# GpSimd's work after the first stage on VectorE, and the softmax products on ScalarE, in a hybrid S5 and attention encoder

## The chip, the cores and the metric

The kernel runs on one core of a Trainium2 chip. The core has five engines with a queue each that is worked off in order: TensorE (PE in the profile; PEld are its weight loads), VectorE (DVE), ScalarE (ACT), GpSimd (POOL) and SyncE (SP), which mostly starts DMAs. Engines wait for each other by semaphores. The metric is the device time of one execution in microseconds, the median of the runs. Lower is better.

## The reference

The input x has 256 tokens of 2048 channels in float32. The trunk has two layers. Layer 0 mixes tokens with a bidirectional S5 state-space mixer that ends in a gated linear unit, `(z @ w_glu_a) * sigmoid(z @ w_glu_b)`. Layer 1 mixes them with grouped-query attention in a window of 128 tokens: 32 query heads of 64 channels share 4 key and value heads, queries and keys are RMS-normalised and rotated, and each head has a sink logit in its softmax. After each mixer follows a squared-ReLU MLP of width 8192. Each of the four parts is `h = h + part(rms_norm(h))`. Cut to the attention core, which matters most here:

```python
qkv = h @ w_qkv
q = apply_rotary(head_rms_norm(q, q_gain), positions)
k = apply_rotary(head_rms_norm(k, k_gain), positions)
scores = einsum(q, k) * 64 ** -0.5, masked to |i - j| <= 128
m = max(max(scores), sink)
p = exp(scores - m)
denom = sum(p) + exp(sink - m)
out = einsum(p / denom, v) @ w_o
```

## The kernel before

Tokens lie on the 128 partitions, in two tiles (`tt` 0 and 1). The residual stays in SBUF (`resid`). All four large parts of the network are matmuls whose weights stream in from HBM once, 1 MB at a time.

*Matmuls in three passes.* A float32 product is made of three fast ones: each operand is split into a rounded high part and the rest, and `mm3` (L717 to L719) adds high x high, low x high and high x low. So each weight tile (`wload`, L665) goes through three steps: a DMA on SyncE's queue into one of two raw buffers; a cast to the high part on ScalarE (L679); and a subtraction that gives the low part (L680). There are three buffers each for high and low parts. The table `whow` (L1289), filled from `QH`, `UH` and `OH` (L39 to L41), says for each tile into how many pieces it is cut and which engine subtracts: each letter is a piece, "v" on VectorE and "g" on GpSimd. In the attention's first product (`QH`, 20 tiles) every other tile from the sixth on is one whole piece on GpSimd; one of the first five tiles of the MLP behind the gated unit (`UH`) is four pieces on GpSimd. The tiles of the gated unit that are named by `WP` are on GpSimd too, and the change leaves them there.

*Norms.* The RMS norm is spread out: `norm_pre` (L731) multiplies a 512-wide block of the residual by the gain (L735) while ScalarE squares and sums it (L737); `norm_post` (L739) transposes the block on PE (L744) and splits it into high and low (L747); the factor 1/rms comes later, from `norm_end`. The gain product is on GpSimd, but for four blocks at the end of the first MLP, for which the caller passes VectorE. `glu_post` (L807) does this for the gated unit, after a sum (L816, L817), the gate (L820, L822) and the residual's sum (L823). At the end of the attention, `fin` (L1262) does it after the residual's sum (L1267).

*Attention.* `proj` (L1179) runs the projection of one head group, 8 query heads at a time with 512 columns: 16 steps of six matmuls, four weight tiles. The keys and values come first, then four groups (`mains`, L1241), then the output projection. While the next group is projected, the heads of the one before run in nine stages for each half of the tokens, at steps given by `HS` (L28). The stages of one half in `attn_head` (L1104):

- `rot`: squares (L1095), their sums and the rsqrt (`head_r`), then the rotary products on VectorE (L1086, L1087) and their sum on GpSimd (`rope`, L1088);
- `turn`: four transposes on PE (L1119), copied by ScalarE (L1121);
- two times `scores`: matmuls (L1130); VectorE adds the mask and finds the maxima (L1134);
- `soft`: maxima and sink (L1143 to L1146, VectorE), eight exponentials with their sums (L1149, ScalarE), the sums' reciprocals (L1150, L1151, VectorE), and eight products of the exponentials with them (L1153, VectorE), 128x256 each;
- `flip` and `mix`: per pair of heads, four transposes of the weights on PE (L1159), a copy by ScalarE (L1161), then the products with the values (L1168); after the last pair the result is split by ScalarE and VectorE (L1173, L1174).

Of the copies by L1161, two buffers exist for each half. PE takes its instructions in order, so a `mix` that waits for its copy holds up the projection matmuls behind it.

*What sets the order.* The code gives an order, but a scheduler in the build then sorts the instructions of each engine by a timeline of its own. So an edit in one place can move instructions of other engines. GpSimd and ScalarE also start DMAs: GpSimd four sums into the residual in each MLP half (L951 to L958) and the loads of the attention's small tables (L1059).

Of the kernel before, what the change touches and what calls it, by code (L numbers as in the profile page):

```python
# [35 lines left out]
WP = range(9, 33)  # L36
WD = 20 + 16 + 64 + 64
FAST = (range(2, 27, 3), (0, 4, 7, 10, 13, 16, 20, 23, 26))
QH = ("v", "vv", "vv", "v") + ("vv", "g") * 8  # L39
UH = ("vv", "vv", "gggg", "vv", "vv")  # L40
OH = ("v",) * 16  # L41


# [134 lines left out]
class Kernel:  # L178
# [549 lines left out]
        self.nc.sync.dma_start(gain, self.gain_src[:, cb * 512:(cb + 1) * 512])  # L728
        return gain

    def norm_pre(self, cb, tt, gain, hg, e=None):  # L731

        nc = self.nc
        r = self.resid[:, tt, cb * 512:(cb + 1) * 512]
        (e or nc.gpsimd).tensor_mul(hg, r, gain)  # L735
        sq = self.tmp.tile([P, 512], F32, name="sq")
        nc.scalar.activation(sq, r, AF.Square, accum_out=self.ss[:, tt, cb:cb + 1])  # L737

# [105 lines left out]
    def mlp(self, nxt, fin):  # L844
        nc, ar = self.nc, self.ar
# [53 lines left out]
        v = nc.vector  # L899
# [34 lines left out]
        def fast(a, w, first, end):  # L934
            for bk, j, g, c in LATE if first else FORMS:
                mm(bk, a, j, w[g], c, stop=end and bk[0] != "x")
# [23 lines left out]
        def end(half, t, j):  # L960
            cb = half * 2 + j
            cs = slice(cb * 512, (cb + 1) * 512)
            v.tensor_add(self.resid[:, t, cs], self.resid[:, t, cs], bks["x%d" % (2 * t + j + 1)])
            if last:
                nc.sync.dma_start(self.d["out"][:, t, cs], self.resid[:, t, cs])
            elif half:
                scaled(t, cb, nc.gpsimd)
                if j:
                    self.norm_end(t)

        def scaled(t, cb, e):
            self.norm_pre(cb, t, gains[:, cb * 512:(cb + 1) * 512], hx[:, t, cb], e)

        atail += [ar.get("at#%d" % i, [1024], F32R, at=49664 + 1024 * i) for i in range(2)]
        nx = split(0, False, True)
# [7 lines left out]
        for half in range(2):  # L983
            bks, begun = {}, set()
            pend = []
            for kp in range(NK):
                a = nx
                if half == 0 and kp == 2:
                    ar.free("at")
                    self.wr[0].add(ar.get("wx#49664", [2048], at=49664))  # L990
                if half and kp == NK - 4:
                    for r in self.wr:
                        r.drop()
                    ar.free("wx")
                    atail[:] = [ar.get("at#%d" % i, [1024], F32R, at=49664 + 1024 * i) for i in range(2)]
                if kp + 1 < NK:
                    nx = split(kp + 1, kp + 1 in FAST[half], kp == 0 if not half else kp + 1 >= NK - 2)
                elif not half:
                    nx = split(0, 0 in FAST[1])
                w = self.wnext() if half or kp else w0  # L1000
                if half and kp == 19 and not last:
                    ar.free("hT#0")
                    hx = ar.get("hx", [2, 4, 512], at=31744)
                    gains = ar.get("hg", [D], at=35840)
                    nc.sync.dma_start(gains, self.d["gains"][nxt])
                    self.ss = self.small.tile([P, 2, 4], F32, name="ss")
                    for t in range(2):
                        for cb in range(2):
                            scaled(t, cb, v)
                if kp in FAST[half]:  # L1010
                    fast(a, w, not begun, kp == FAST[half][-1])
                    if kp == FAST[half][-1]:
                        fold()
                elif kp < NK - 1 - half:
                    for b in range(4):
                        plain(a, w, b)
                else:
                    pend.append((a, w))
            if half:
                ar.free("hT", "af")  # L1020
                if not last:
                    self.act = ar.get("act", [KT, 2, L], F32R, at=23552)
            n = half and not last
            for t in range(2):
                for p in pend[:n]:
                    for j in range(2):
                        plain(*p, 2 * t + j)
                for j in range(2):
                    for p in pend[n:]:
                        plain(*p, 2 * t + j, stop=p is pend[-1])  # L1030
                    end(half, t, j)
# [46 lines left out]
    def rope(self, pool, src, n, x, tt):  # L1078

        v = self.nc.vector  # L1080
        t1 = pool.tile([P, n, 2, 32], F32, name="rp_a") if n == 8 else self.tmp.tile([P, n, 2, 32], F32, name="gain")
        t2 = pool.tile([P, n, 2, 32], F32, name="rp_b", bufs=1) if n == 8 else self.tmp.tile([P, n, 2, 32], F32, name="sq")
        sv = src.rearrange("p (n s c) -> p n s c", n=n, s=2)
        A = self.ropeA[:, x, tt].rearrange("p (o s c) -> p o s c", o=1, s=2).broadcast_to([P, n, 2, 32])
        B = self.ropeB[:, x, tt].rearrange("p (o s c) -> p o s c", o=1, s=2).broadcast_to([P, n, 2, 32])
        v.tensor_mul(t1, sv, A)  # L1086
        v.tensor_mul(t2, sv[:, :, ::-1], B)  # L1087
        self.nc.gpsimd.tensor_add(t1, t1, t2)  # L1088
        return t1.rearrange("p n s c -> p (n s c)")

    def head_r(self, pool, src, n, tt, scale, name):
# [12 lines left out]
    def attn_head(self, pool, g, banks):  # L1104

        nc, v, a, pe = self.nc, self.nc.vector, self.nc.scalar, self.nc.tensor
        kT, vt = self.kT, self.vt

        def stages(tt):
# [27 lines left out]
            def soft():  # L1137
                mx, sm = s["mx"], s["sm"]
                snk = self.sink[:, g * 8:(g + 1) * 8]
                nm = self.small.tile([P, 8], F32, name="nm")  # L1140
                es = self.small.tile([P, 8], F32, name="es")
                den = self.small.tile([P, 8], F32, name="den")
                v.tensor_mul(mx, mx, s["r"])  # L1143
                v.tensor_max(mx, mx, snk)
                v.tensor_scalar_mul(nm, mx, -1.0)
                v.tensor_add(es, snk, nm)  # L1146
                a.activation(es, es, AF.Exp)
                for h in range(8):
                    a.activation(sm[:, h], sm[:, h], AF.Exp, scale=s["r"][:, h:h + 1], bias=nm[:, h:h + 1], accum_out=den[:, h:h + 1])  # L1149
                v.tensor_add(den, den, es)  # L1150
                v.reciprocal(den, den)  # L1151
                for h in range(8):
                    v.tensor_scalar_mul(sm[:, h], sm[:, h], den[:, h:h + 1])  # L1153

            def flip(hp):
                bk = self.bank()
# [129 lines left out]
    def run(self):  # L1286
        nc, d, ar = self.nc, self.d, self.ar
        self.wq = []
        self.whow = {**{163 - j: h for j, h in enumerate(QH)}, **{143 - j: h for j, h in enumerate(OH)}, **{291 - j: h for j, h in enumerate(UH)}}  # L1289
        self.wsrc = ([d["wge"][c, k] for c in (1, 2, 3, 0) for k in range(KT // 2)] + [None] + [d["wgl"][c, k] for c in range(4) for k in range(KT // 4)]  # L1290
# [219 lines left out]
```

## Time and profile before

| what | value |
|---|---|
| median of three runs | 2092.61 us (2088.96 to 2093.38) |
| profiled execution | 2089.93 us, its span 2088.1 us |
| PE busy | 2013.2 us (96%) |
| VectorE busy | 1476.5 us (71%) |
| ScalarE busy | 1091.0 us (52%) |
| GpSimd busy | 338.5 us (16%) |
| HBM read | 360.05 MB, 173 GB/s over the span |

The stages in the timeline: the S5 mixer to about 200 us, the gated unit to about 390, the first MLP to about 1095, the attention to about 1390, the second MLP to the end.

In the rows of the profile, "L680 DVE TENSOR_TENSOR slot<-slot,slot" is the work of line 680 on VectorE, output before the arrow. In the timeline the first number is the start in us from the span's start, the second the time until the last of the row's instructions ended; a bracket at the end tells how long the engine stood idle before and what ended that. Successive instructions of one engine overlap a little, so that the distance of two starts is often shorter than a duration. Matmuls of 512 columns last 0.39 us in the rows while starting 0.227 us apart. In a table of waits a row gives the waiting line, what it waited for, the total in us, the number of times and the longest.

### The profile page before, as it was taken

To read this page: it belongs to the slowest core of one execution; us is meant where nothing else is said; L and a number is where in the kernel's file an instruction comes from. 1 tells how busy PE (TensorE), PEld (TensorE's weight loads), DVE (VectorE), ACT (ScalarE), POOL (GpSimd) and SP (SyncE) were. 2 spreads that over 40 slices of the span, in tenths; PEclk is the share of its full clock that TensorE was granted. 3 is DMA by queue.
4 is the path that set the end of the run, shared out by engine and by line. 5 is a ranking of instruction groups with operands and counts; after the bars stand their busy time and mean duration, and the time that the engine had idled before them with its cause. 6 is when DMAs were issued, how large, how long until landed. Compare 5 with 4: busy or idle time off the path is not lost.

```text
span 2088.1 us, 33141 instructions
## 1 busy us (share of the span) xinstructions
PE 2013.2 (96%) x13736; PEld 1693.2 (81%) x13736; DVE 1476.5 (71%) x2096; ACT 1091.0 (52%) x1314; POOL 338.5 (16%) x260
## 2 busy tenths in 40 slices
PE   5989999899999999999999889999999999999999
PEld 4877778788888888878787667888888888787887
DVE  8899636755555578988886877465555557898886
ACT  5553645444444455655554556454444445565553
POOL 6988721200000000000022430100000000000000
PEclk9999999999999999999999999999999999999999
DMA  3224455455555555465564332455555555547554
GB/s 120 71 98 145 153 194 200 166 197 187 196 182 193 191 196 207 181 222 207 198 206 172 121 121 81 149 186 200 193 190 184 197 185 198 204 182 241 182 205 158
DMA packets 61990, 368.47 MB, mean 176 GB/s; under 512 B 7072, under 2 KB 9408, under 8 KB 21904
## 3 DMA queue, kind: packets, MB, share of 16 engines
q1 hardware_dynamic: 54144, 342.32, 46.0%
q10 hardware_dynamic: 5184, 19.49, 2.7%
q0 software_dynamic: 2512, 4.56, 1.2%
q8 instruction: 107, 1.75, 0.3%
q14 instruction: 43, 0.35, 0.0%
HBM read 360.05 MB, written 2.10 MB: 173 GB/s over the span
## 4 chain that ended last, share of the span: by engine, by line
PE 62%; DVE 9%; DMA 7%; ACT 3%; issue 2%; POOL 0%; SPq 0%; ACTq 0%; DVEq 0%
PE bank L858 22%; PE bank L924 22%; PE bank L860 12%; DMA slot<-in_wdn 4%; DVE slot L680 4%; PE bank L717 2%; PE bank L718 1%; PE bank L719 1%; ACT slot L679 1%; DVE slot L694 1%; ACT slot L693 1%; DMA slot<-in_wup 1%; DMA slot<-in_wo 1%; ACT slot L1149 1%; PE bank L1168 1%
## 5 line engine op out<-in xcount | busy, mean ns | idle before, releaser
L680 DVE TENSOR_TENSOR slot<-slot,slot 128x2048 fp32r<-128x2048 f32 (+1 forms) x285 | 628.8, 2209 | 417.2 <-ACT slot L679 414.6
L679 ACT CAST slot<-slot 128x2048 fp32r<-128x2048 f32 (+2 forms) x321 | 554.6, 1733 | 466.5 <-PE bank L858 195.1
L924 PE MATMUL bank<-slot,slot 128*128 128x512 f32 x2124 | 493.4, 390 | 2.5 <-DVE slot L918 1.8
L858 PE MATMUL bank<-slot,slot 128*128 128x512 f32 x2048 | 492.4, 392 | 2.8 <-DVE slot L747 1.6
L924 PEld LDWEIGHTS bank<-slot,slot 128*128 128x128 f32 x2124 | 397.7, 188 | 88.4 <-DVE slot L918 4.2
L858 PEld LDWEIGHTS bank<-slot,slot 128*128 128x128 f32 x2048 | 377.0, 189 | 76.5 <-DVE slot L747 2.2
L860 PEld LDWEIGHTS bank<-slot,slot 128*128 128x128 f32 x2048 | 263.1, 191 | 10.3
L860 PE MATMUL bank<-slot,slot 128*128 128x256 f32 x2048 | 266.3, 283 | 0.0
L717 PE MATMUL bank<-slot,slot 128*128 128x512 f32 x544 | 219.2, 404 | 5.2 <-ACT slot L679 4.9
L719 PE MATMUL bank<-slot,slot 128*128 128x512 f32 x544 | 209.5, 398 | 7.3 <-POOL slot L680 7.1
L718 PE MATMUL bank<-slot,slot 128*128 128x512 f32 x544 | 215.5, 396 | 0.0
L924 PE MATMUL bank<-slot 128*128 128x512 f32 x840 | 201.1, 391 | 4.1 <-DVE slot L918 3.4
L951 POOL DMA_DIRECT2D slot<-slot x4 | 3.7, 921 | 1159.0 <-ACT slot L950 1149.3
L924 PEld LDWEIGHTS bank<-slot 128*128 128x128 f32 x840 | 157.0, 188 | 40.2 <-DVE slot L918 6.5
L694 DVE TENSOR_TENSOR slot<-slot,slot 128x1536 fp32r<-128x1536 f32 x72 | 145.5, 2021 | 39.5 <-ACT slot L693 36.4
L693 ACT CAST slot<-slot 128x1536 fp32r<-128x1536 f32 x72 | 122.3, 1698 | 93.3 <-DMA slot<-in_wdn 46.5
L869 ACT ACTIVATE slot<-slot 128x256 f32<-128x256 f32 x128 | 52.8, 414 | 159.0 <-DVE slot L867 159.0
L717 PEld LDWEIGHTS bank<-slot,slot 128*128 128x128 f32 x544 | 104.0, 191 | 30.0 <-ACT slot L679 6.1
L719 PEld LDWEIGHTS bank<-slot,slot 128*128 128x128 f32 x544 | 102.8, 191 | 31.4 <-POOL slot L680 9.1
L718 PEld LDWEIGHTS bank<-slot,slot 128*128 128x128 f32 x544 | 103.9, 191 | 20.8 <-issue 0.7
L917 ACT CAST slot<-slot 128x512 fp32r<-128x512 f32 (+1 forms) x128 | 90.5, 709 | 53.5 <-PE bank L924 52.9
L680 POOL TENSOR_TENSOR slot<-slot,slot 128x1024 fp32r<-128x1024 f32 (+2 forms) x36 | 100.6, 2808 | 104.6 <-ACT slot L679 98.9
(238 smaller groups left out, 1800.0 us busy)
## 6 DMA issues: line engine op xcount, KB each, us to landing
slot<-in_wup SPq DMA_DIRECT2D x128, 1024.0 KB, 4.9
slot<-in_wdn SPq DMA_DIRECT2D x128, 1024.0 KB, 4.9
slot<-in_wqkv SPq DMA_DIRECT2D x20, 1024.0 KB, 5.0
slot<-in_wge ACTq DMA_DIRECT2D x32, 512.0 KB, 3.8
slot<-in_wgl SPq DMA_DIRECT2D x16, 1024.0 KB, 5.3
slot<-in_wo SPq DMA_DIRECT2D x16, 1024.0 KB, 4.9
slot<-in_bz SPq DMA_DIRECT2D x16, 336.0 KB, 3.3
slot<-in_cp SPq DMA_DIRECT2D x16, 256.0 KB, 2.7
```

The lines of the kernel that those rows point to most:

```text
L679: self.nc.scalar.copy(hi[:, c], raw[:, c])
L680: (self.nc.gpsimd if e == "g" else self.nc.vector).tensor_sub(lo[:, c], raw[:, c], hi[:, c].bitcast(F32))
L693: self.nc.scalar.copy(hi, x)
L694: v.tensor_sub(lo, x, hi.bitcast(F32))
L717: pe.matmul(out, lhsT=xh, rhs=wh, start=first, stop=False)
L718: pe.matmul(out, lhsT=xl, rhs=wh, start=False, stop=False)
L719: pe.matmul(out, lhsT=xh, rhs=wl, start=False, stop=last)
L858: pe.matmul(bk, lhsT=wh[:, kt], rhs=act[:, kt].rearrange("p x c -> p (x c)"), start=(kt == 0), stop=False)
L860: pe.matmul(bk[:, :L], lhsT=wl[:, kt], rhs=act[:, kt, 0], start=False, stop=(kt == KT - 1))
L869: nc.scalar.activation(o if fb % 2 else o[:, ::-1], s.rearrange("p (x c) -> p x c", x=2), AF.Square)
L917: nc.scalar.copy(a[:, :c], h)
L924: pe.matmul(bank(bk), lhsT=a[x][:, j], rhs=w[y][:, c], start=bk not in begun, stop=stop and y == 1)
```

## The change

Three things, all after the first stage (the S5 mixer):

- the subtractions that the tables `QH` and `UH` gave to GpSimd go to VectorE: eight whole tiles of 128x2048 in the attention, and one tile in the gated unit's end that is now cut into two pieces instead of four;
- the gain products (L735, 128x512: eight in the gated unit, four at the first MLP's end, eight at the attention's end) and the rotary sums (L1088: eight of 128x512 and two of 128x256) go from GpSimd to VectorE;
- the 64 products of the exponentials with the reciprocal sums (L1153, 128x256) go from VectorE to ScalarE.

GpSimd keeps in these stages four copies of keys (L1230) and its DMAs.

```diff
-QH = ("v", "vv", "vv", "v") + ("vv", "g") * 8
-UH = ("vv", "vv", "gggg", "vv", "vv")
+QH = ("v", "vv", "vv", "v") + ("vv", "v") * 8
+UH = ("vv", "vv", "vv", "vv", "vv")
...
-    def norm_pre(self, cb, tt, gain, hg, e=None):
+    def norm_pre(self, cb, tt, gain, hg):
...
-        (e or nc.gpsimd).tensor_mul(hg, r, gain)
+        nc.vector.tensor_mul(hg, r, gain)
...
-                scaled(t, cb, nc.gpsimd)
+                scaled(t, cb)
...
-        self.nc.gpsimd.tensor_add(t1, t1, t2)
+        v.tensor_add(t1, t1, t2)
...
-                    v.tensor_scalar_mul(sm[:, h], sm[:, h], den[:, h:h + 1])
+                    a.mul(sm[:, h], sm[:, h], den[:, h:h + 1])
```

More of the change, by code (lines that the diff above doesn't have):

```diff
@@ L966, in end, with scaled @@
             elif half:
-                scaled(t, cb, nc.gpsimd)
+                scaled(t, cb)
                 if j:
                     self.norm_end(t)
-        def scaled(t, cb, e):
-            self.norm_pre(cb, t, gains[:, cb * 512:(cb + 1) * 512], hx[:, t, cb], e)
+        def scaled(t, cb):
+            self.norm_pre(cb, t, gains[:, cb * 512:(cb + 1) * 512], hx[:, t, cb])
         atail += [ar.get("at#%d" % i, [1024], F32R, at=49664 + 1024 * i) for i in range(2)]
@@ L1008, in mlp @@
                         for cb in range(2):
-                            scaled(t, cb, v)
+                            scaled(t, cb)
                 if kp in FAST[half]:
```

## The prediction

> **What bounds the kernel now.** I read the page's busy line first, then the table of waits by engine, then the stage where PE waits most, row by row. One fence after another comes from: the page; a table of stretches (length, then busy time of each engine, granted clock, DMA); PE's waits in four stretches; and the timeline.
>
> ```profile
> PE 2013.2 (96%) x13736; PEld 1693.2 (81%) x13736; DVE 1476.5 (71%) x2096; ACT 1091.0 (52%) x1314; POOL 338.5 (16%) x260
> ```
> ```profile
> 1130.00:1310.00 180.00, 162.75 (x909) 125.15 (x908) 136.11 (x397) 102.90 (x214) 52.12 (x20) 0.94 0.30 109
> ```
> ```profile
> PE bank L717 <- ACT slot L679: 3.5, 1, 3.5
> PE bank L719 <- POOL slot L680: 3.0, 2, 2.0
> PE bank L1119 <- POOL slot L1088: 0.3, 1, 0.3
> ```
> ```profile
> PE bank L1168 <- DVE mx L1134: 4.7, 1, 4.7
> PE bank L1159 <- DVE slot L1153: 4.0, 2, 2.5
> PE bank L719 <- POOL slot L680: 1.0, 1, 1.0
> PE bank L1168 <- ACT slot L1161: 0.4, 1, 0.4
> ```
>
> PE works 96% of the span, so the change can only move the waits of PE. Among the stages it touches, attention holds nearly all: 6.8 us in the first list (1080 to 1180 us) and 10.1 us in the second (1180 to 1320), 16.9 us together. A second loss lies in the granted clock, 0.94 over 180 us: 180 x 0.06 = 10.8 us. It follows waits, as these PE rows show (start, duration): behind the wait of 2.0 us before 1138, projection matmuls start 0.43 us apart; undisturbed, 0.227 us.
>
> ```profile
> 1139.41 0.63 PE L719 MATMUL bank<-slot,slot 128*128 128x512 f32 x1
> 1139.84 0.63 PE L717 MATMUL bank<-slot,slot 128*128 128x512 f32 x1
> ...
> 1260.55 0.39 PE L718 MATMUL bank<-slot,slot 128*128 128x512 f32 x1
> 1260.77 0.39 PE L719 MATMUL bank<-slot,slot 128*128 128x512 f32 x1
> ```
>
> Four waits are 2 us or longer (3.5, 2.0, 4.7, 2.5), so I charge 10.8 / 4 = 2.7 us of slow clock to each, and none to shorter ones. The Trainium skill (TensorE: Matmul & The Clock Gate, What's actually happening) has the clock fall only after an idle window of about 3.4 us; the 2.0 us wait contradicts that here. By its rule only two of the old waits and three of the new ones below would be charged, and the sum at the end would be +3.4 us, not -2.0 us.
>
> Why PE waits is seen on VectorE: the same eight multiplications by reciprocal sums (L1153) take three times as long while GpSimd subtracts.
>
> ```profile
> 1217.53 6.47 DVE L1153 TENSOR_SCALAR slot<-slot,den 128x256 f32<-128x256 f32 x8
> ...
> 1265.22 2.19 DVE L1153 TENSOR_SCALAR slot<-slot,den 128x256 f32<-128x256 f32 x8
> ```
> ```profile
> 1218.98 4.60 POOL L680 TENSOR_TENSOR slot<-slot,slot 128x2048 fp32r<-128x2048 f32 x1 [11.76 <-ACT slot L679]
> ```
>
> The excess, 4.3 us, is about GpSimd's 4.60 us: VectorE stands still meanwhile. Of the 16.9 us only the 2.5 us wait at 1265 (no GpSimd work near it) and the 0.4 us one are free of this; 14.0 us could go.
>
> **The change part by part.** *Subtractions, rotary sums, norm products to VectorE.* Prices (a group of GpSimd rows, then one VectorE row of each size):
>
> ```profile
> L680 POOL TENSOR_TENSOR slot<-slot,slot 128x2048 fp32r<-128x2048 f32 x8 | 38.5, 4811 | 66.2 <-ACT slot L679 66.2
> L735 DVE TENSOR_TENSOR slot<-slot,slot 128x512 f32<-128x512 f32 x4 | 2.5, 684 | 0.0
> ```
> ```profile
> 1226.67 1.22 DVE L680 TENSOR_TENSOR slot<-slot,slot 128x1024 fp32r<-128x1024 f32 x1
> ```
>
> Eight whole-tile subtractions cost VectorE 8 x 2 x 1.22 = 19.5 us at most, eight rotary sums 8 x 0.68 = 5.5 us; they replace GpSimd's 38.5 us for the former alone, during which VectorE was held. Between 1130 and 1310 VectorE was busy 136 us of 180; it loses most of the 52 us that GpSimd held it and the multiplications. So VectorE has room, and in attention I cost this part at nothing; without the cover its 25 us would be the price. The norm products of the layer ends (20 x 0.68 us) fall where PE has other matmuls, but for one place, the end of the gated unit. On VectorE (names: output<-inputs, slot_73 the small ring) before:
>
> ```order
> L816 TENSOR_TENSOR slot_313<-slot_313,bank 128x512
> L822 TENSOR_TENSOR slot_73<-slot_313,slot_73 128x512
> L823 TENSOR_TENSOR slot_73<-slot_73 128x512
> L822 TENSOR_TENSOR slot_73<-slot_313,slot_73 128x512
> L680 TENSOR_TENSOR slot_2734<-slot_82,slot_4069 128x1024
> ```
> and now:
> ```order
> L816 TENSOR_TENSOR slot_313<-slot_313,bank 128x512
> L680 TENSOR_TENSOR slot_2733<-slot_82,slot_4069 128x1024
> L822 TENSOR_TENSOR slot_73<-slot_313,slot_73 128x512
> L680 TENSOR_TENSOR slot_2734<-slot_82,slot_4069 128x1024
> L823 TENSOR_TENSOR slot_73<-slot_73 128x512
> L822 TENSOR_TENSOR slot_73<-slot_313,slot_73 128x512
> L735 TENSOR_TENSOR slot_73<-slot_73 128x512
> ```
>
> Two half subtractions and one more L822 now stand ahead of the first norm product, for which PE's transposes wait (3.94 us below).
>
> ```profile
> 387.48 0.68 DVE L817 TENSOR_TENSOR slot<-slot,bank 128x512 f32<-128x512 f32 x1
> 388.07 0.68 DVE L816 TENSOR_TENSOR slot<-slot,bank 128x512 f32<-128x512 f32 x1
> ```
> ```profile
> 394.18 0.66 PE L744 MATMUL bank<-ident,slot 128*128 128x128 f32 x4 [3.94 <-POOL slot L735]
> ```
>
> From the first L817 to PE: 6.70 us now. After: five short operations at 0.60 apart, a half subtraction 1.2, L822 0.6, another half 1.2, L823 and L822 1.2, L735 0.68 = 7.9 us. **+1.2 us.**
>
> *Multiplications to ScalarE.* ScalarE has such products only 512 wide (L347, the eighth starts 4.3 us after the first, so 0.61 apart); two other ScalarE operations, 512 and 256 wide, differ by 0.21 us.
>
> ```profile
> L347 ACT ACTIVATE slot<-slot,rstd x8: 705/708/722, 65.3 to 69.6; 128x512 f32<-128x512 f32 x8
> ```
> ```profile
> 409.40 0.62 ACT L917 CAST slot<-slot 128x512 fp32r<-128x512 f32 x1
> ...
> 417.33 0.41 ACT L869 ACTIVATE slot<-slot 128x256 f32<-128x256 f32 x1
> ```
>
> So 0.61 - 0.21 = 0.40 us each, 3.2 us for eight (0.50 each if they don't overlap), against 2.19 us on VectorE. What counts is who is behind them. ScalarE in the third head group, first half, before (L1149 exponentials, L679 weight cast, L1095 squares, L1161 copies of transposed weights):
>
> ```order
> L1149 ACTIVATE slot_4602,den<-slot_4602,nm,slot_4603 128x256 x5
> L1095 ACTIVATE slot_73<-bank,rstd 128x512
> L679 CAST slot_4069<-slot_82 128x2048
> L1095 ACTIVATE slot_73<-bank,rstd 128x512
> L1161 COPY slot_4603<-bank 128x512
> ```
> and now:
> ```order
> L1149 ACTIVATE slot_4602,den<-slot_4602,nm,slot_4603 128x256 x5
> L679 CAST slot_4069<-slot_82 128x2048
> L1153 ACTIVATE slot_4602<-slot_4602,den 128x256 x8
> L1095 ACTIVATE slot_73<-bank,rstd 128x512
> L679 CAST slot_4069<-slot_82 128x2048
> L1095 ACTIVATE slot_73<-bank,rstd 128x512
> L1161 COPY slot_4603<-bank 128x512
> ```
>
> The first copy (L1161), which releases the product with the values (L1168) on PE, now stands behind eight products and a second cast. The reciprocals come from VectorE while the first cast runs, so they add no wait. Durations:
>
> ```profile
> 1259.34 0.60 ACT L1149 ACTIVATE slot<-slot,nm,slot 128x256 f32<-128x256 f32 x1 [2.36 <-DVE nm L1145]
> ...
> 1264.12 0.67 ACT L1095 ACTIVATE slot<-bank,rstd 128x512 f32<-128x512 f32 x1
> 1264.69 1.89 ACT L679 CAST slot<-slot 128x2048 fp32r<-128x2048 f32 x1
> 1266.48 0.68 ACT L1095 ACTIVATE slot<-bank,rstd 128x512 f32<-128x512 f32 x1
> 1267.06 1.20 ACT L1161 COPY slot<-bank 128x512 f32<-128x512 f32 x2
> ```
>
> From starts: exponentials 4.78, cast 1.79, products 3.2, square 0.57, cast 1.79, square 0.58, copy 0.58: 13.3 us from the first exponential. On PE, before:
>
> ```order
> L1130 MATMUL bank<-slot_4603,slot_9706 128x256 x8
> L1159 MATMUL bank<-ident,slot_4602 128x128 x8
> L1168 MATMUL bank<-slot_4603 64x128 x4
> L1159 MATMUL bank<-ident,slot_4602 128x128 x8
> L717 MATMUL bank<-slot_4069,slot_9432 128x512
> ```
> and now:
> ```order
> L719 MATMUL bank<-slot_2733,slot_4067 128x512
> L717 MATMUL bank<-slot_4069,slot_4067 128x512
> L718 MATMUL bank<-slot_4069,slot_4067 128x512
> L719 MATMUL bank<-slot_2733,slot_4067 128x512
> L1159 MATMUL bank<-ident,slot_4602 128x128 x8
> L1168 MATMUL bank<-slot_4603 64x128 x4
> L1159 MATMUL bank<-ident,slot_4602 128x128 x8
> ```
>
> Nine projection matmuls now stand between the scores (L1130) and the transposes (L1159), where there were none. PE's durations, from start to start, and when VectorE starts on scores (the trace records each L1130 and L1168 twice, so x16 and x8 there are x8 and x4 in the order):
>
> ```profile
> 1218.03 1.15 PE L1159 MATMUL bank<-ident,slot 128*128 128x128 f32 x8 [1.49 <-DVE slot L1153]
> 1218.94 0.47 PE L719 MATMUL bank<-slot,slot 128*128 128x512 f32 x1
> ...
> 1255.10 0.66 PE L1168 MATMUL bank<-slot,slot 128*64 128x128 f32 x8
> 1255.70 0.66 PE L1119 MATMUL bank<-ident,slot 128*128 128x128 f32 x4
> 1256.11 0.47 PE L717 MATMUL bank<-slot,slot 128*128 128x512 f32 x1
> ...
> 1261.09 2.00 PE L1130 MATMUL bank<-slot,slot 64*128 64x256 f32 x16
> ```
> ```profile
> 1255.38 0.42 DVE L1134 CUSTOM_DVE_ANT_0 slot<-bank,slot 128x256 f32<-128x256 f32 x1
> ...
> 1262.26 0.42 DVE L1134 CUSTOM_DVE_ANT_0 slot<-bank,slot 128x256 f32<-128x256 f32 x1 [2.75 <-PE bank L1130]
> ```
>
> The first exponential came 4.2 us after the end of the scores (1255.10 to 1259.34) with VectorE late; unhindered, VectorE starts 0.8 us before that end (1262.26 against 1263.09) and needs 3.4 (1255.38 to 1259.34, less 0.6 for one operation between), so 2.5 us. I take 3.2, between. The copy is then done 3.2 + 13.3 = 16.5 us after the scores. PE's own work until it wants the copy, with the projection matmuls (0.227 us each) counted in the new order:
> - third group: four L1168 0.60, transposes 0.41, 22 projections 5.0, scores 2.0, nine projections 2.0, transposes 0.91 = 11.0. Wait **5.5**.
> - first: no L1168, 14 projections instead of nine: 11.5. Wait **5.0**.
> - second: one projection more than the first, and L1168: 12.3. Wait **4.2**.
> - fourth: both score sets at once, 41 and 22 projections between: 18.4; ScalarE has 16 exponentials (9.6), products, two casts (3.6), copy: 20.1. Wait **1.7**.
>
> In the first and second the second cast is two halves; I price them as one. New waits 16.4, slow clock 3 x 2.7 = 8.1: 24.5 us, against 16.9 + 10.8 = 27.7. Attention: **-3.2 us**. With the gated unit: **-2.0 us**.
>
> The Trainium skill (ScalarE: Activation LUTs, Rules for kernel authors) would leave products on VectorE. Here 2.19 us against 3.2 us bears it out once GpSimd is out of the way. It speaks against this half of the change: without these products in ScalarE's queue each of the four waits would be up to 3.2 us shorter.
>
> **The rivals.** *The relief carries* (0.28). VectorE's early finish makes the first exponential come sooner and the new waits vanish in PE's slack, all 14.0 us and three slow clocks (8.1) go: -22.1 + 1.2, 2071.7 us. For it: ScalarE was busy only 103 us of 180. Against it: the copy's place in the queue is fixed. *ScalarE becomes the bound* (0.22), the other side. Per group it has 9.6 exponentials, 6.4 products, four casts 7.2, eight copies of about 0.58 and eight more short operations, some 32 us; PE has 96 x 0.227 = 21.8 and twice about 6.5 of attention, some 35. If ScalarE idles for more than those 3 us in a group, the second half's transposes wait too: 3.2 + 2.7 in three groups, +17.7, 2108.3 us. That the change doesn't take GpSimd out cannot be: its rows there are gone but for key copies and DMAs.
>
> **How the numbers follow.** The profiled execution took 2089.93 us (span 2088.1), 2.7 below the median of the runs, 2092.61; I carry the difference of -2.0 over to the median: 2090.6 us. Chance of this case 0.50. Its ends: exponentials at 4.2 instead of 3.2 (+4.0, and a slow clock in the fourth group, +2.7), products at 0.50 (+3.2): 2100.5; exponentials at 2.5 (-2.8), slow clock of 1.8 instead of 2.7, three times: 2085.1. A measurement of this kernel tells no change from about 0.2%, 4.2 us. Case one gives faster 0.09, same 0.36, slower 0.05; the relief 0.26 and 0.02 same; the bound 0.03 same and 0.19. Sum: faster 0.35, same 0.41, slower 0.24. The range takes in case one and reaches into both rivals, 2079 to 2104.
>
> **What would show it.** Right: no GpSimd row in attention but copies and DMAs; VectorE's halves at 1.2 us throughout; PE waiting for L1161 at L1168 three times for 4 to 6 us, and for L735 at the gated unit's end for 5 us. Wrong: these waits missing (relief), or as many again at the second half's L1159 (bound). A clock at 0.97 or more over attention would also say that my charge of 2.7 us was too high.

## The result, and the profile after

The changed kernel takes 2079.09 us, median of 5 runs (2075.13 to 2082.94), against 2092.82 us (2088.96 to 2095.3, 5 runs) for the kernel before: ratio 0.9935, 95% interval 0.9915 to 0.9956. It is 13.7 us faster; 2.0 were forecast, 2090.6 us. The profiled execution of the changed kernel has a span of 2074.6 us, 13.5 less than before, so the two traces show all of the difference. The busy line of its page:

```profile
PE 2004.5 (97%) x13736; PEld 1688.0 (81%) x13736; DVE 1455.1 (70%) x2072; ACT 1116.2 (54%) x1376; POOL 246.1 (12%) x218
```

PE has the same 13736 matmuls as before and is busy 8.7 us less with them; the other 4.8 us are idle time. To find where, I cut both traces at matmuls that occur in both, and took the distances:

| stretch (from, to) | before | after | difference |
|---|---|---|---|
| span's start to first L858 of the first MLP | 385.45 | 384.11 | -1.3 |
| first L858 to first L924 (end of the gated unit in it) | 365.52 | 360.53 | **-5.0** |
| first L924 to the L744 ahead of the attention | 346.44 | 346.75 | +0.3 |
| that L744 to the next one (attention) | 244.70 | 238.39 | **-6.3** |
| that L744 to the last L765 (start of the second MLP) | 54.42 | 53.23 | **-1.2** |
| from there to the end | 691.57 | 691.59 | 0.0 |

The first row is scatter: the fourteen profiles of this study have its end anywhere between 384.1 and 390.3 us. The second repeats better: five of the seven kernels that share the changed kernel's code there have 360.5 us, and the other two (e4 and e8 below) take 1.6 and 1.3 us more, behind a slow clock of which the last section tells. So the stretches in bold can be trusted more than whole times.

*Attention.* Its stretch as a row of the stretches' view, in the kernel before and in the changed one (length, then PE, PEld, DVE, ACT, POOL, the granted clock, DMA share and GB/s):

```profile
1097.41:1342.11 244.70, 227.44 (x1253) 177.48 (x1252) 171.46 (x453) 131.66 (x248) 60.05 (x24) 0.96 0.34 123
```
```profile
1091.39:1329.78 238.39, 223.75 (x1254) 176.38 (x1253) 142.05 (x410) 156.67 (x312) 2.53 (x4) 0.96 0.36 127
```

Read them as length less PE's busy time: PE was idle 17.3 us before and 14.6 after (-2.6), and busy 227.4 and 223.8 with the same matmuls (-3.7). The second part is the slow clock: the same instructions take less time. The clock column, with two digits, is too coarse to show it. By the stretches in which the granted clock is 0.50, PE was busy 19.2 us at half clock before and 12.5 us after; half of the difference is 3.4 us. What PE waits for after the change, from its timeline:

```profile
1167.18 1.13 PE L1168 MATMUL bank<-slot 128*64 128x128 f32 x8 [4.25 <-ACT slot L1161]
...
1209.77 1.13 PE L1168 MATMUL bank<-slot 128*64 128x128 f32 x8 [3.31 <-ACT slot L1161]
...
1252.72 1.13 PE L1168 MATMUL bank<-slot 128*64 128x128 f32 x8 [4.57 <-ACT slot L1161]
...
1298.61 0.66 PE L1168 MATMUL bank<-slot 128*64 128x128 f32 x8 [0.88 <-ACT slot L1161]
...
1309.45 0.66 PE L1168 MATMUL bank<-slot 128*64 128x128 f32 x8 [1.44 <-ACT slot L1161]
```

Every wait behind GpSimd, VectorE's products and the masked scores is gone. In their place stands the one wait that was forecast, the products with the values (L1168) behind the copy (L1161), once in each head group.

*End of the gated unit.* Two rows of PE before, beside the wait of 3.94 us that the prediction shows, and three after:

```profile
394.59 4.58 PE L858 MATMUL bank<-slot,slot 128*128 128x512 f32 x12
...
402.43 1.21 PE L858 MATMUL bank<-slot,slot 128*128 128x512 f32 x4 [1.40 <-DVE slot L747]
```
```profile
384.11 2.88 PE L858 MATMUL bank<-slot,slot 128*128 128x512 f32 x12
...
391.12 0.66 PE L744 MATMUL bank<-ident,slot 128*128 128x128 f32 x4 [2.70 <-DVE slot L735]
391.53 3.00 PE L858 MATMUL bank<-slot,slot 128*128 128x512 f32 x12
```

The wait at L744 fell to 2.70 us, the wait of 1.40 us behind it is gone, and the twelve matmuls after it take 3.00 us, near the 2.88 of undisturbed ones, where they took 4.58 at the slow clock. At the start of the second MLP a wait of 1.21 us, before, has gone as well:

```profile
1388.91 1.20 PE L858 MATMUL bank<-slot,slot 128*128 128x512 f32 x4 [1.21 <-DVE ms L755]
```
```profile
1375.39 1.20 PE L858 MATMUL bank<-slot,slot 128*128 128x512 f32 x4
```

### The profile page after: what moved, and what is told of

It is laid out like the page before. It is cut to its first block, busy times and chain, and to the rows that moved or that the text cites. A ratio compares the mean times of both kernels' runs of the same rounds, so it can differ in the third digit from the quotient of the medians.

```text
span 2074.6 us, 33114 instructions
## 1 busy us (share of the span) xinstructions
PE 2004.5 (97%) x13736; PEld 1688.0 (81%) x13736; DVE 1455.1 (70%) x2072; ACT 1116.2 (54%) x1376; POOL 246.1 (12%) x218
## 4 chain that ended last, share of the span: by engine, by line
PE 69%; DVE 6%; DMA 4%; ACT 4%; issue 2%; DVEq 0%; ACTq 0%
PE bank L858 22%; PE bank L924 21%; PE bank L860 12%; DMA slot<-in_wdn 4%; PE bank L719 4%; PE bank L717 4%; PE bank L718 4%; DVE slot L680 2%; DVE slot L694 1%; ACT slot L1149 1%; ACT slot L693 1%; PE bank L1168 1%; ACT slot L679 1%; PE bank L1159 1%; DVE slot L918 1%
## 5 line engine op out<-in xcount | busy, mean ns | idle before, releaser
L680 DVE TENSOR_TENSOR slot<-slot,slot 128x2048 fp32r<-128x2048 f32 (+1 forms) x295 | 639.4, 2169 | 425.4 <-ACT slot L679 413.2
L679 ACT CAST slot<-slot 128x2048 fp32r<-128x2048 f32 (+1 forms) x319 | 554.5, 1743 | 460.6 <-PE bank L858 190.1
L924 PE MATMUL bank<-slot,slot 128*128 128x512 f32 x2124 | 493.3, 390 | 3.7 <-DVE slot L918 1.9
L858 PE MATMUL bank<-slot,slot 128*128 128x512 f32 x2048 | 490.2, 391 | 0.1
L924 PEld LDWEIGHTS bank<-slot,slot 128*128 128x128 f32 x2124 | 397.8, 188 | 89.6 <-DVE slot L918 4.1
L858 PEld LDWEIGHTS bank<-slot,slot 128*128 128x128 f32 x2048 | 376.0, 188 | 72.8 <-DVE ms L755 0.3
L924 PE MATMUL bank<-slot 128*128 128x512 f32 x840 | 201.1, 391 | 3.1 <-DVE slot L918 2.2
L924 PEld LDWEIGHTS bank<-slot 128*128 128x128 f32 x840 | 156.8, 188 | 39.4 <-DVE slot L918 5.8
L918 DVE TENSOR_TENSOR slot<-slot,slot 128x512 fp32r<-128x512 f32 (+1 forms) x128 | 101.7, 797 | 1.4 <-ACT slot L917 0.7
```

The costliest lines, as they stand in the source:

```text
L679: self.nc.scalar.copy(hi[:, c], raw[:, c])
L680: (self.nc.gpsimd if e == "g" else self.nc.vector).tensor_sub(lo[:, c], raw[:, c], hi[:, c].bitcast(F32))
L858: pe.matmul(bk, lhsT=wh[:, kt], rhs=act[:, kt].rearrange("p x c -> p (x c)"), start=(kt == 0), stop=False)
L918: v.tensor_sub(a[:, n:n + c], h, a[:, :c].bitcast(F32))
L924: pe.matmul(bank(bk), lhsT=a[x][:, j], rhs=w[y][:, c], start=bk not in begun, stop=stop and y == 1)
```

## The experiments

In all of them one place of the code differs from the kernel before or from the changed one. *Queue theory* is the prediction's: in attention, the waits are set by what stands in ScalarE's queue ahead of the first copy L1161, and GpSimd's work held VectorE. Each ratio is to the kernel before on the same chip, with its 95% interval. Stretches are those of the table above.

**e1: GpSimd's work moved, the products left on VectorE** (from the changed kernel).

```diff
-                    a.mul(sm[:, h], sm[:, h], den[:, h:h + 1])
+                    v.tensor_scalar_mul(sm[:, h], sm[:, h], den[:, h:h + 1])
```

> The changed kernel with the eight products (L1153) back on VectorE; all of GpSimd's work stays moved. Queue theory (ScalarE's queue, with 3.2 us of products in front of the first L1161 copy, makes the waits of 14.4 us at L1168): those waits fall to under 6 us in sum, and the kernel takes 2066 to 2073 us, ratio to before 0.988 to 0.9905, against 0.9935 for the change. Rival (the order that the scheduler chooses decides, not who multiplies; VectorE then owes 2.2 us of products ahead of the transposes, L1159): the waits move from L1161 to L1153 with about the same sum of 12 to 16 us, and the ratio stays at 0.9925 to 0.9955.

Measured: 0.9940 (0.9926 to 0.9954), attention 236.8 us: no different from the changed kernel. PE's waits:

```profile
1168.43 0.66 PE L1168 MATMUL bank<-slot 128*64 128x128 f32 x8 [1.22 <-ACT slot L1161]
...
1212.10 1.94 PE L1159 MATMUL bank<-ident,slot 128*128 128x128 f32 x8 [7.47 <-DVE slot L1153]
...
1216.93 1.12 PE L1168 MATMUL bank<-slot 128*64 128x128 f32 x8 [2.90 <-ACT slot L1161]
...
1258.26 0.66 PE L1168 MATMUL bank<-slot 128*64 128x128 f32 x8 [2.06 <-ACT slot L1161]
```

Both theories are half right. In the first and third group PE has as many projection matmuls between scores and transposes as in the changed kernel (14 and 9), and there the wait falls from 4.25 to 1.22 and from 4.57 to 2.06: 3.0 and 2.5 us, a little less than the 3.3 us of the products on ScalarE. In the second group the scheduler now puts none there, where the changed kernel has 14, and PE waits 7.47 + 2.90 us instead of 3.31. The sum of waits, 14.2 us, is near the changed kernel's 14.5.

**e2: only the products moved to ScalarE** (from the kernel before, the reverse of the edit above).

> The kernel before with only the products (L1153) moved to ScalarE; GpSimd keeps its subtractions, rotary sums and norm products. Queue theory: the waits behind GpSimd stay (3.5, 2.0, 1.0, 4.7 us at L679, L680 and L1134), the 4.0 us behind L1153 go, and 8 to 14 us behind L1161 come; ratio 1.000 to 1.006. Rival (freeing VectorE of the products is a gain of its own): fewer waits in sum than the 16.9 us before, ratio 0.994 to 0.998.

Measured: 1.0049 (1.0034 to 1.0064), attention 254.1 us, 9.4 longer. The ratio is the queue theory's, its waits are so in part (a table of PE's waits over attention):

```profile
PE bank L1168 <- ACT slot L1161: 15.0, 5, 9.3
PE bank L1159 <- ACT slot L1153: 3.8, 2, 3.2
PE bank L717 <- ACT slot L679: 3.5, 1, 3.5
PE bank L1119 <- POOL slot L1088: 3.1, 1, 3.1
PE bank L719 <- POOL slot L680: 2.1, 2, 1.1
```

The waits behind L1161 are a little above the 8 to 14 us expected. The 4.7 us behind the masked scores, expected to stay, are gone, and 3.8 us behind the products came. As the prediction had it, this half of the change is a loss by itself, of 9.4 us in attention.

**e3: only attention's GpSimd work moved to VectorE** (from the kernel before).

```diff
-QH = ("v", "vv", "vv", "v") + ("vv", "g") * 8
+QH = ("v", "vv", "vv", "v") + ("vv", "v") * 8
...
-        self.nc.gpsimd.tensor_add(t1, t1, t2)
+        v.tensor_add(t1, t1, t2)
```

> The kernel before with only attention's GpSimd work moved to VectorE (half of the weight subtractions L680 and the rotary sums L1088); products stay on VectorE, the gated unit's end and the norm products stay on GpSimd. Queue theory with VectorE held by GpSimd: 14.0 of the 16.9 us of waits in attention go and most of 10 us of slow clock with them, so attention is 10 to 18 us shorter, ratio 0.991 to 0.995. Rival (VectorE's own 25 us of new work comes out uncovered, or the scheduler's new order makes other waits): attention within 4 us of before, ratio 0.998 to 1.002.

Measured: 0.9972 (0.9961 to 0.9983); attention 238.4 us, 6.3 less than before, between the two expectations. The stretch's row:

```profile
1099.02:1337.41 238.39, 223.22 (x1253) 175.12 (x1252) 158.75 (x471) 132.11 (x248) 5.12 (x6) 0.96 0.36 126
```

Its length is that of the changed kernel: GpSimd's absence alone gives attention's whole gain, and the products on ScalarE add nothing to it. That the two agree to the hundredth is chance, since their waits are others. The relief did not come to 10 us or more since other waits took the place of the old ones: 7.5 us behind the products in the second group, as in e1, and 7.3 us in sum behind L1161.

**e4: only the end of the gated unit and the norm products moved** (from the kernel before). It makes both edits below; **e5** makes the first alone, **e6** the second.

```diff
-UH = ("vv", "vv", "gggg", "vv", "vv")
+UH = ("vv", "vv", "vv", "vv", "vv")
...
-        (e or nc.gpsimd).tensor_mul(hg, r, gain)
+        nc.vector.tensor_mul(hg, r, gain)
```

> The kernel before with only the end of the gated unit (L680 of its last tile) and the norm products (L735) moved to VectorE; attention as before. By the forecast's own step for this place (+1.2 us): ratio 0.9995 to 1.0015. Rival, as the two traces differ outside attention (7.7 us shorter between the first L858 of each MLP and its full speed: 1.2 + 1.6 us of waits and about 1.6 us of slow clock at the first, 1.2 us at the second and what follows from it): ratio 0.995 to 0.9975, attention's waits as before.

> The kernel before with only the four quarter subtractions at the end of the gated unit (third entry of UH) moved from GpSimd to VectorE; norm products stay on GpSimd. Theory A (VectorE stood still while GpSimd subtracted, from 386 to 391 us, and that delayed the gated unit's last operations): most of what e4 showed at that place comes with this edit alone, PE's wait at L744 falls from 3.9 to under 3 us, the stretch from the first L858 to the first L924 from 365.5 to 361 to 363 us, ratio 0.997 to 0.9985. Theory B (the forecast's step: the two half subtractions go ahead of the norm product in VectorE's queue and cost 1.2 us): the wait grows to about 5 us, ratio 1.000 to 1.0015.

> The kernel before with only the norm products (L735) moved from GpSimd to VectorE; the subtractions of UH and attention stay. Theory A: the wait at L744 falls by about the difference of one product, 1.8 against 0.7 us, to 2.5 to 3 us; the second wait there (1.4 us at L858) and the one of 1.2 us at the second layer's start go too; ratio 0.998 to 0.9995. Theory B (it is this half that made e4's gain, since a norm product on GpSimd holds VectorE between the rstd operations): ratio 0.9965 to 0.998, as e4.

Measured: e4 0.9974 (0.9962 to 0.9985), e5 1.0006 (0.9995 to 1.0016), e6 0.9976 (0.9967 to 0.9986). The stretch of the gated unit's end, 365.5 us before, is 362.1 in e4, 366.0 in e5 and 359.7 in e6; attention keeps 244.5 to 245.8. PE at that place in e4, e5 and e6:

```profile
391.11 0.66 PE L744 MATMUL bank<-ident,slot 128*128 128x128 f32 x4 [2.71 <-DVE slot L735]
391.52 4.59 PE L858 MATMUL bank<-slot,slot 128*128 128x512 f32 x12
```
```profile
397.89 1.12 PE L744 MATMUL bank<-ident,slot 128*128 128x128 f32 x4 [4.37 <-POOL slot L735]
398.66 5.34 PE L858 MATMUL bank<-slot,slot 128*128 128x512 f32 x12
```
```profile
392.33 0.66 PE L744 MATMUL bank<-ident,slot 128*128 128x128 f32 x4
392.74 3.01 PE L858 MATMUL bank<-slot,slot 128*128 128x512 f32 x12
...
399.16 1.19 PE L858 MATMUL bank<-slot,slot 128*128 128x512 f32 x4 [1.54 <-DVE slot L747]
```

So at this place the forecast's step falls (e4), and theory B holds in e5 (a wait of 4.37 us, where about 5 were expected) and e6: the norm products alone make the gain. Moving the subtractions alone (e5) gains nothing and costs 0.5 us here; with the norm products on VectorE they bring the wait at L744 back (from none to 2.7) and take the later one of 1.54 away, 0.8 us by the stretch of the changed kernel (360.53 against 359.73).

**e7: each product made twice on ScalarE** (from the changed kernel; the weights are scaled twice).

```diff
-                for h in range(8):
+                for h in [*range(8)] * 2:
                     a.mul(sm[:, h], sm[:, h], den[:, h:h + 1])
```

> The changed kernel with each product (L1153) made twice on ScalarE, so the weights are scaled twice: 3.2 us more in ScalarE's queue for each half of a group. On PE the first half of the first group keeps its order (scores, 14 projection matmuls, transposes, L1168). Queue theory: the wait of 4.25 us there grows by 3.2 us to 7 to 8 us, and the waits for L1161 in sum by 8 to 13 us; ratio to before 0.998 to 1.005. Rival (ScalarE has slack ahead of the copies, what sets the wait is VectorE's softmax operations): that wait stays at 4 to 5 us, ratio 0.993 to 0.996.

Measured: 1.0034 (1.0020 to 1.0047), attention 255.6 us. PE in the first group:

```profile
1167.75 1.97 PE L1159 MATMUL bank<-ident,slot 128*128 128x128 f32 x8 [2.96 <-ACT slot L1153]
...
1177.88 1.13 PE L1168 MATMUL bank<-slot 128*64 128x128 f32 x8 [8.16 <-ACT slot L1161]
```

The 4.25 us have become 2.96 + 8.16, 6.9 more, where 3.2 were expected. ScalarE's queue tells the rest: between the products and the first copy the scheduler has now put the other half's eight exponentials too. Over all of attention the waits behind L1161 grew by only 1 us, to 15.5, where 8 to 13 were expected; 10.0 us behind the products (L1153) and 2.7 us behind a cast came beside them. The rival, slack on ScalarE, falls; but the price of one operation in the queue is not its duration alone.

**e8: casts of every other weight tile on VectorE** (from the changed kernel).

```diff
-QH = ("v", "vv", "vv", "v") + ("vv", "v") * 8
+QH = ("v", "vv", "vv", "v") + ("vv", "w") * 8
...
-                self.nc.scalar.copy(hi[:, c], raw[:, c])
+                (self.nc.vector.tensor_copy if e == "w" else self.nc.scalar.copy)(hi[:, c], raw[:, c])
```

> The changed kernel with the casts (L679) of every other weight tile from the queries on made by VectorE as well, with their subtraction behind. It takes 1.8 us per such tile off ScalarE's queue, where one of them stood in front of the first L1161 copy. Queue theory: the waits for L1161 of 14.4 us in sum fall by about 1.8 us in three groups, to 7 to 11 us, ratio 0.989 to 0.993. Rival (VectorE, with 71 of 130 us busy, becomes late in its turn, or the scheduler puts other ScalarE work into the room): waits of 13 us or more in sum, ratio 0.993 to 0.998.

Measured: 0.9975 (0.9965 to 0.9986), attention 241.2 us. The rival holds: with a cast gone from ScalarE's queue, the scheduler put the other half's eight exponentials (4.8 us) ahead of the first copy in the first two groups, and the waits there grew; in the third, where it did not, the wait fell from 4.57 to 2.96 us. The waits behind L1161 are 17.1 us in sum. The first two groups:

```profile
1175.59 1.13 PE L1168 MATMUL bank<-slot 128*64 128x128 f32 x8 [6.33 <-ACT slot L1161]
...
1219.40 1.13 PE L1168 MATMUL bank<-slot 128*64 128x128 f32 x8 [5.10 <-ACT slot L1161]
```

**e9: the changed kernel with the gated unit's subtractions back on GpSimd** (`UH` as before).

> The changed kernel with the four quarter subtractions at the end of the gated unit (third entry of UH) given back to GpSimd; all else as in the changed kernel. What e5 and e6 show together (norm products on VectorE gain about 5 us there, the subtractions on VectorE then cost some of it): the wait of 2.7 us at L744 goes, the stretch from the first L858 to the first L924 is 1 to 3 us shorter than the 360.5 us of the changed kernel. The scheduler's order in the second group changes too (one projection matmul between scores and transposes, not 14), for which 3 us more of waits are expected there, so the whole comes out near the changed kernel, ratio to before 0.992 to 0.996. Rival (the stretch varies by that much from run to run, and the two edits don't interact): stretch within 0.5 us of 360.5.

Measured: 0.9960 (0.9945 to 0.9975). That stretch is 359.8 us, as in e6, 0.7 less than in the changed kernel: less than expected, nearer the rival. Attention became 4.1 us longer (242.5), by an edit that lies 700 us ahead of it: the scheduler moved 13 projection matmuls away from between scores and transposes in the second group, as the expectation says.

**e10: products of the second half of the tokens back on VectorE** (from the changed kernel).

```diff
-                    a.mul(sm[:, h], sm[:, h], den[:, h:h + 1])
+                    if tt == 0:
+                        a.mul(sm[:, h], sm[:, h], den[:, h:h + 1])
+                    else:
+                        v.tensor_scalar_mul(sm[:, h], sm[:, h], den[:, h:h + 1])
```

> The changed kernel with the products (L1153) of the second half of the tokens back on VectorE, and those of the first half left on ScalarE. PE keeps about the order of the changed kernel in the first halves (14, 12, 8 and 41 projection matmuls between scores and transposes, there 14, 14, 9 and 41). If the order that the scheduler makes decides: the four waits behind L1161 stay at 3 to 5 us each in the first three groups and no wait of 7.5 us behind L1153 comes, ratio to before 0.992 to 0.995. If ScalarE's load as such decides: attention 3 us shorter or more than the changed kernel's, ratio under 0.992.

Measured: 0.9976 (0.9967 to 0.9986), attention 244.7 us. Neither: the first two groups wait 4.25 and 3.72 us as expected, but in the third the scheduler again put the other half's exponentials ahead of the copy:

```profile
1266.41 1.13 PE L1171 MATMUL bank<-slot 128*64 128x128 f32 x8 [9.35 <-ACT slot L1164]
```

**e11: softmax in two parts of four heads, products on VectorE** (from the changed kernel, `UH` as before). **e12: the same two parts, products on ScalarE in the first two groups only** (`UH` as in the changed kernel). The diff is e12's; e11 has its last line for all groups.

```diff
-                for h in range(8):
-                    a.activation(sm[:, h], sm[:, h], AF.Exp, scale=s["r"][:, h:h + 1], bias=nm[:, h:h + 1], accum_out=den[:, h:h + 1])
-                v.tensor_add(den, den, es)
-                v.reciprocal(den, den)
-                for h in range(8):
-                    a.mul(sm[:, h], sm[:, h], den[:, h:h + 1])
+                for q in range(0, 8, 4):
+                    for h in range(q, q + 4):
+                        a.activation(sm[:, h], sm[:, h], AF.Exp, scale=s["r"][:, h:h + 1], bias=nm[:, h:h + 1], accum_out=den[:, h:h + 1])
+                    hs = slice(q, q + 4)
+                    v.tensor_add(den[:, hs], den[:, hs], es[:, hs])
+                    v.reciprocal(den[:, hs], den[:, hs])
+                    for h in range(q, q + 4):
+                        if g < 2:
+                            a.mul(sm[:, h], sm[:, h], den[:, h:h + 1])
+                        else:
+                            v.tensor_scalar_mul(sm[:, h], sm[:, h], den[:, h:h + 1])
```

> The changed kernel with each half's softmax made in two parts of four heads (exponentials, reciprocal sums and products of heads 0 to 3, then of 4 to 7), products on VectorE, and the gated unit's quarter subtractions on GpSimd. The first copy L1161 then stands ahead of one square and one cast more than before in the first group, with no products in ScalarE's queue; in the second group the scheduler has no projection matmul between scores and transposes. Queue theory: first and third group's waits for L1161 under 1.5 us each, the second group's wait behind the softmax 5 to 8 us; attention 233 to 237 us, gated unit's stretch 358 to 360 us, ratio to before 0.989 to 0.992: the best of all. Rival (the sum of waits stays where it is, since the scheduler only moves them): attention 238 us or more, ratio 0.992 to 0.996.

> The changed kernel with each half's softmax made in two parts of four heads, and the products (L1153) on ScalarE in the first two head groups only, on VectorE in the last two. For the first two groups PE keeps the changed kernel's order, with 14 projection matmuls between scores and transposes each; for the last two it has that of e11. If the order of PE and ScalarE's queue together set the waits: about 4.2 and 3.3 us behind L1161 in the first two groups, under 1 us in the third and fourth (there 4.6 and 2.3 us in the changed kernel); attention 229 to 233 us, ratio to before 0.988 to 0.991, the fastest of all. If the scheduler only moves the waits about: attention 236 us or more, ratio 0.992 to 0.996.

Measured: e11 0.9920 (0.9906 to 0.9934), attention 236.1 us; e12 0.9895 (0.9878 to 0.9911), 2070.11 us, attention 228.3 us. PE's waits over attention in e11, as a table, and in e12, with the row of its stretch (line numbers are shifted by the edit: L1161 and L1155 in e11 are transposes and products, L1163 and L1166 the copy, L1170 and L1173 the products with the values):

```profile
PE bank L1161 <- DVE slot L1155: 9.6, 2, 9.3
PE bank L1170 <- ACT slot L1163: 4.8, 1, 4.8
PE bank L1130 <- ACT slot L1121: 0.7, 1, 0.7
```
```profile
PE bank L1173 <- ACT slot L1166: 7.9, 3, 4.3
```
```profile
1095.99:1324.27 228.28, 220.19 (x1254) 174.41 (x1253) 151.94 (x458) 144.77 (x280) 3.14 (x4) 0.99 0.38 133
```

In e11 the first, third and fourth group wait for no copy, as expected; nearly all that is left is the second group, where PE has no projection matmul between scores and transposes: 9.28 + 4.80 us, where 5 to 8 were expected. Its attention is in the range of the queue theory, its ratio at the edge between that and the rival's. e12 gives that group the changed kernel's order and keeps e11's for the last two: waits of 4.27, 3.34 and 0.29 us, as expected, idle time 8.1 us instead of 14.6, and a clock of 0.99. e11 can't be told from the changed kernel by its ratio. e12's interval lies below the changed kernel's, so e12 is faster than that, and 22 us faster than the kernel before. No run has the choice by group without the split in two parts, so what each of the two gives by itself stays open.

## Where the prediction was right, and where it failed

The measured 2079.09 us lies 11.5 us below the forecast of 2090.6, and within the range of 2079 to 2104 by a tenth of a microsecond. That it is inside is luck: the scatter of the first stretch alone, 1.3 us here, is larger. The forecast's direction was right, its size was not.

- **Attention (-3.2 forecast, -6.3 measured).** The mechanism of the waits was right: they moved from GpSimd and VectorE to L1161 behind ScalarE's queue, 5.0, 4.2, 5.5 and 1.7 us forecast, 4.25, 3.31, 4.57 and 0.88 + 1.44 measured. Two sizes were a little off. The start of the exponentials was taken 3.2 us after the scores; in the first two groups it came 2.7 after, near the lower end of 2.5. And the slow clock cost 3.7 us less of PE's busy time, where 2.7 (one wait of four) were charged; the charge of 2.7 us for each wait from 2 us on is not how the clock falls, as the last section shows. The sum by the rule of a whole idle window, +3.4 us, was also worked out wrongly: if only two of the old waits had made the 10.8 us, each would have cost 5.4, and three such new ones give +6.1. The products' price, 0.40 us each, 3.2 for eight, was met:

```profile
1160.32 3.30 ACT L1153 ACTIVATE slot<-slot,den 128x256 f32<-128x256 f32 x8
```

- **VectorE takes GpSimd's work at no cost in attention.** Right, by e3: VectorE's busy time there fell from 171.5 to 158.8 us although it does more.
- **The gated unit's end (+1.2 forecast, -5.0 measured).** This step failed. The queue that I costed was right: from the first L817 to PE's L744 it was 7.9 us by the forecast and is 8.03 (383.09 to 391.12), and the subtractions alone cost 0.5 to 0.8 us (e5, e9). What failed is the sentence that "the norm products of the layer ends fall where PE has other matmuls, but for one place", and that at this place only what is added to VectorE's queue counts. I took the product's own stay on GpSimd as given. e6 shows that it was the cost: with nothing else moved, the wait at L744 is gone and the stretch 5.8 us shorter. The sign that I named, a wait of 5 us for L735, did not come; it was 2.70. On GpSimd the product took 1.77 us, for 0.68 on VectorE, and what runs ahead of it was late: the first L817 began 2.0 us after PE's first L858 before, and 1.0 us ahead of it after the change. Of the waits of 3.94 and 1.40 us and 1.6 us of slow clock, 2.70 us are left. That no slow clock follows the 2.70 us is in part luck: it followed an equal wait there in e4 and in e8. The product before, on GpSimd, and the chain's two ends after, on VectorE:

```profile
392.35 1.77 POOL L735 TENSOR_TENSOR slot<-slot 128x512 f32<-128x512 f32 x1 [1.35 <-DVE slot L823]
```
```profile
383.09 0.68 DVE L817 TENSOR_TENSOR slot<-slot,bank 128x512 f32<-128x512 f32 x1
...
390.38 0.68 DVE L735 TENSOR_TENSOR slot<-slot 128x512 f32<-128x512 f32 x1
```

- **The second MLP's start (nothing forecast, -1.2 measured).** The same sentence failed here, but the cause is not settled. In e6, as in the changed kernel, the wait of 1.21 us behind L755 is gone. It is gone in e3 too, which leaves the norm products on GpSimd and has 0.3 us of wait left there; so either edit is enough.
- **The products on ScalarE are a loss by themselves.** Right (e2, +0.49%); but the changed kernel with them on VectorE is no faster (e1), against "without these products each of the four waits would be up to 3.2 us shorter". That held for the two groups in which the scheduler kept PE's order, and was given back in the one where it didn't. The Trainium skill's advice (ScalarE: Activation LUTs, Rules for kernel authors) to keep such products on VectorE is thus borne out by e2 and by the first and third group of e1, and hidden in e1's time by the order in the second. In e12's last two groups the products are on VectorE as well, but the softmax is split there too, so they don't show it alone.
- **The rivals.** "The relief carries" had its size from waits that vanish; they did not, since ScalarE's queue was there, as its own counter-argument said. "ScalarE becomes the bound" did not come: no second half's transposes wait. The time lies at the low end of the range because the term of the gated unit's end had the wrong sign (6.2 of the 11.5 us), attention gained 3.1 us more than forecast and the second MLP's start 1.2, not because either rival came.

What stays open: why ScalarE's and VectorE's operations ahead of the gated unit's end ran some 3 us earlier against PE once the norm products had left GpSimd. The trace before shows a cast there that waited 3.8 us for its weights, which fits buffers that come free late behind a held VectorE. But in e6 the same cast still waits 2.85 us, and no run isolates it.

## What to carry to other kernels

Ask of an operation on a slow engine not only what its new place costs but what its old place holds up: moving twenty products of 0.7 us off GpSimd was worth 5 us (e6). Where a scheduler orders the instructions, read the new order of every engine before pricing a change of engine: here the same products on ScalarE cost 3 us of waits in one head group and saved 7 in another, by how many projection matmuls stood between scores and transposes. Choosing the engine group by group together with the softmax in two parts (e12) gave another 0.4%.

## What the runs showed of the hardware

GpSimd does not hold all of VectorE. While GpSimd subtracted at the gated unit's end before the change, VectorE's sums with one operand in PSUM (L816, L817, bank) took their usual 0.68 us, and the product of two SBUF operands beside them 1.68 for 0.68:

```profile
385.97 5.03 POOL L680 TENSOR_TENSOR slot<-slot,slot 128x512 fp32r<-128x512 f32 x4 [8.21 <-ACT slot L679]
```
```profile
389.86 1.68 DVE L822 TENSOR_TENSOR slot<-slot,slot 128x512 f32<-128x512 f32 x1
```

This agrees with the Trainium skill (SBUF — State Buffer, Who interferes with whom): an operation with at most one SBUF input, outside the two-port modes, doesn't contend, one with two does.

The same wait can cost the slow clock or not. Behind 2.71 us at L744 in e4 twelve matmuls took 4.59 us; behind 2.70 us at the same place in the changed kernel 3.00. The traces show why. The granted clock changes only between stretches of 3.41 us that follow each other without regard to the waits: it is 0.50 for one of them or for several in a row, else 1.00. Here are e4 and then the changed kernel, cut at these stretches (length, then busy time of PE and the others, the granted clock after POOL's column):

```profile
388.30:391.71 3.41, 0.70 (x6) 0.61 (x6) 3.41 (x7) 0.97 (x3) 0.00 (x0) 1.00 0.80 296
391.71:395.12 3.41, 3.41 (x10) 2.63 (x9) 3.35 (x23) 1.19 (x3) 0.00 (x0) 0.50 0.01 2
```
```profile
386.88:390.29 3.41, 1.54 (x13) 1.33 (x11) 3.27 (x5) 1.36 (x3) 0.00 (x0) 1.00 0.56 178
390.29:393.70 3.41, 2.58 (x14) 2.20 (x15) 3.35 (x15) 1.56 (x6) 0.00 (x0) 1.00 0.31 130
```

In e4 the whole wait falls into one stretch, PE is idle for 79% of it, and the next stretch runs at half clock. In the changed kernel an equal wait is divided between two stretches, idle for 55% and 24%, and the clock stays. Cut so, the fourteen traces hold 48 falls of the clock between 300 us and the last 8 us: PE was idle for 49% or more of the stretch before each, and wherever it was idle for 58% or more the clock fell; between 49% and 57% it fell six times of fifteen. The Trainium skill (TensorE: Matmul & The Clock Gate, What's actually happening) has a window of about 3.4 us that runs freely, not from a wait's start. The trace agrees with that, at 3.41 us; that a whole window must be idle, as the skill asks, it does not bear out, since 58% was enough. A charge per wait, like my 2.7 us, can only be an average.
